# A two-layer encoder trunk: last query tile's 528 scores in one two-bank PSUM tile, 16-column meta scores, and a rearranged end of layer A

## The chip, the cores and the metric

One core of one Trainium2 chip runs the whole kernel in one launch. The metric is device time in microseconds; lower is better. The profile is one execution taken by the hardware profiler.

## The reference, cut to what matters

The input is 512 frames of 1024 features; 16 meta tokens are put in front, so L = 528. Layer A is differential attention (8 heads, two score maps a head, d = 64) and a conv-gated FFN; layer B is latent attention (16 heads, 64 plain and 32 rotary dimensions) and a second FFN. A frame sees its own chunk of 64 frames, the earlier chunks and the meta tokens; a meta token sees the 16 meta tokens alone.

```python
# layer A, per head                       # layer B, per head
a = softmax(q1 k1.T / 8)                  p = softmax((qn kn.T + qr kr.T) * 96**-0.5)
a = a - lam * softmax(q2 k2.T / 8)        o = p @ v
o = rms_norm(a @ v, g_sub) * (1 - lam_init)
h = h + concat(o) @ w_o;  h = h + conv_ffn(h)      # in both layers
```

## The kernel before, in words

Everything is float32. Each dense product is done in three TensorE passes of reduced-precision operands: every weight and activation is split into a high part (ScalarE, `act.copy`) and a low part (VectorE or GpSimd, a subtraction), and `mm3` (L162) issues high*high, high*low, low*high, each as a weight load and a matmul over 264 columns (half of L). Apart from stretches under `tc.manual_schedule`, the order of the instructions on each engine is not the program's: a planner goes through the program with its own estimate of durations and gives each engine, at each moment, the ready instruction of the highest priority, which is the earliest in the program (`soon(n)` moves a block n instructions forward). The order is fixed at build; on the chip each engine works through its queue in that order, and tiles that share a buffer wait for each other.

**Scores.** `scores` (L381) makes three steps for one head (layer B) or one map of a head (layer A). There are four query tiles of 128 rows, with 144, 272, 400 and 528 visible keys. The negated row maximum is a VectorE `tensor_reduce` (`negmax`, L391), the exponential a ScalarE `activation` that also returns the row sum (`ex`, L396). A PSUM bank holds 512 floats a partition, so the 528 keys of the last tile are cut in 256 and 272: `s0` puts tile 0 and the 256 in bank `b0`, the 272 in bank `b1`, joins the two maxima with a `min` (L410), and takes three exponentials; `s2` adds the two row sums (L428). `s1` puts the 400 keys of tile 2 in `b2` and, in its columns 400 to 415, the 16 meta scores: q of tokens 0 to 127 against the 16 meta keys, of which rows 0 to 15 are used. `s2` is tile 1 in `b3`. The four banks come from a pool of three (`psS`, tag "s"). One `qk` is two matmuls in layer A and three in layer B, each with its own weight load.

**Layer A's loop (L709).** For head h: `attend_a(h)` (scores of both maps, value projection `vproj(h)`, subtraction of the maps with L600, ten transposes L609 and four L623, values L630 and L631, squares and sums), then `qkproj(h + 1)`. `finish_a(h0, h1)` (L648) scales the outputs of heads h0 to h1-1 by their root mean square, transposes them and splits them into `oh` and `ol`. The root is on GpSimd (13 small instructions, `rsqrt`) where `soft` is true, else on ScalarE with Sqrt. `meta_soft_a` and `meta_a` do the meta tokens' rows. With KA = 5, `finish_a(4, 5)` stands after head 5 and `finish_a(5, 7)` after head 6; the meta rows go in groups of heads 0 to 3, 4, and 5 to 7. In the last head an activation with Sqrt on one column of the row sums (L588) stands ahead of `meta_soft_a(5, 3)`, which uses Exp, and `meta_a(5, 3)` stands at the end of `attend_a` (L639). ScalarE loads another table when the function changes between Exp and Sqrt.

**Output projection (L730).** Part 1 is the sum over heads 0 to KA-1 for the eight output tiles, in two halves each, 15 matmuls a PSUM bank; part 2 is heads KA to 7 and prepares the FFN's input tile by tile (L263). Both take banks from `psD`, which has two. Part 1 has the lowest priority of what surrounds it, so it fills TensorE where the attention leaves it free. `wload2` loads and splits weights for two output tiles at a time, in pieces of up to 512 columns.

Layer B (L1239) goes head by head: `s0`, values of head h-2, `s1`, transposes of head h-1, `s2`, with projections as fill.

Of the kernel before, what the change touches and what calls it, by code (L numbers as in the profile page):

```python
# [10 lines left out]
F32 = mybir.dt.float32  # L11
# [3 lines left out]
ALU = mybir.AluOpType  # L15
# [20 lines left out]
KA = KB = 5  # L36
# [21 lines left out]
def tile_trunk(ctx, tc, out, h0, gan0, small, w_qkv, a_w_o, kv_w_dkv, kv_w_ukv, b_w_dq, b_w_uq,  # L58
# [286 lines left out]
    first_ps = [[takeD() for _ in range(2)], [psS.tile([P, 512], F32, tag="s", name="psk") for _ in range(2)]]  # L345
# [35 lines left out]
    def scores(psS, ap_, parts, row, smeta, ebufs=2):  # L381
# [5 lines left out]
        def qk(ps, q0, k0, n):  # L387
            for i, (q, k) in enumerate(parts):
                pe.matmul(ps, q[:, q0:q0 + P], k[:, k0:k0 + n], start=i == 0, stop=i == len(parts) - 1)  # L389
# [9 lines left out]
        bank = lambda n: psS.tile([P, 512], F32, tag="s", name=n)  # L399

        def s0():
            b0 = bank("b0")
            qk(b0[:, 0:256], 16, 0, 256)
            qk(b0[:, 256:512], 400, 0, 256)
            negmax(b0[:, 0:144], 0, 80)
            negmax(b0[:, 256:512], 3)
            b1 = bank("b1")
            qk(b1[:, 0:272], 400, 256, 272)
            negmax(b1[:, 0:272], 4, 208)
            dve.tensor_tensor(nm[:, 3:4], nm[:, 3:4], nm[:, 4:5], ALU.min)  # L410
            ex(b0[:, 0:144], J0[0], 0, 0)
            ex(b0[:, 256:512], J0[3], 3, 3)
            ex(b1[:, 0:272], J0[3] + 256, 3, 4)

        def s1():
            b2 = bank("b2")
            qk(b2[:, 0:400], 272, 0, 400)
            qk(b2[:, 400:416], 0, 0, NM)
            negmax(b2[:, 0:400], 2, 336)
            dve.tensor_copy(smeta[:, row, :], b2[:NM, 400:416])  # L420
            ex(b2[:, 0:400], J0[2], 2, 2)

        def s2():
# [4 lines left out]
            dve.tensor_tensor(su[:, 3:4], su[:, 3:4], su[:, 4:5], ALU.add)  # L428
# [55 lines left out]
    some = iter([psT.tile([P, 512], F32, tag="t", name="psr"), psS.tile([P, 512], F32, tag="s", name="psr")])  # L484
# [92 lines left out]
    def attend_a(h, qs, ks, kl, vs0=None):  # L577
# [8 lines left out]
        if h == HA - 1:  # L586

            act.activation(s1a[:, 0, 0:1], es[1][1][:, 3:4], AF.Sqrt)  # L588
            ms = meta_soft_a(KA, 8 - KA)
# [8 lines left out]
        for j in (0, 3, 2, 1):  # L598
            sl = slice(J0[j], J0[j] + JN[j])
            dve.scalar_tensor_tensor(e1[:, sl], e2[:, sl], cc[:, j:j + 1], e1[:, sl], ALU.mult, ALU.add)  # L600

# [36 lines left out]
        if h == HA - 1:  # L638
            meta_a(KA, 8 - KA, *ms, soft=False)  # L639

# [68 lines left out]
    for h in range(HA):  # L709
# [8 lines left out]
        if h == 5:  # L718
            finish_a(4, KA)
            meta_a(4, KA - 4, *meta_soft_a(4, KA - 4))  # L720
        if h == 6:
            finish_a(KA, 7)
# [732 lines left out]
```

## Time and profile before

| | |
|---|---|
| median of 3 runs | 1312.9 us (1310.15 to 1313.72) |
| the profiled execution: time, span | 1312.65 us, 1310.8 us |
| TensorE matmul busy | 1279.3 us |
| VectorE, ScalarE, GpSimd busy | 814.4, 619.9, 206.1 us |
| layer A's attention, about | 36 to 297 us of the span |
| first FFN; latent products | 297 to 690; 690 to 737 us |
| layer B's attention and output | 737 to 938 us |
| second FFN and end | 938 to 1311 us |

Times are counted from the start of the span. PE is TensorE, PEld its weight loads (which overlap the matmuls), DVE VectorE, ACT ScalarE, POOL GpSimd. A matmul's record is longer than its pace: the distance from one start to the next says what it takes. The granted clock is 1.00 at 2.4 GHz and 0.50 at 1.2 GHz.

### The profile page before, as it was taken

The page shows a single profiled execution, that of the slowest core. Times are in us where ns is not written, and L with a number is a line of the kernel's source. Part 1 is how long each engine was busy: PE and PEld are TensorE (multiplying, and loading weights), DVE is VectorE, ACT ScalarE, POOL GpSimd, SP SyncE. Part 2 cuts the span into 40 slices and gives each one's busy share as a digit, 9 for nine tenths or more (in the row PEclk, how much of TensorE's full clock was granted, in tenths as well). Part 3 has the DMA queues.
Part 4 walks back from the last instruction along what each step waited for, and adds up shares of the span by engine and source line. Part 5 has one row for each costly group of instructions (what it writes and reads, how often), then busy time and mean ns, then how long its engine had stood idle before and what let it go on. Part 6 is the DMA issues. An engine that isn't in the chain of part 4 may idle for free.

```text
span 1310.8 us, 23833 instructions
## 1 busy us (share of the span) xinstructions
PE 1279.3 (98%) x9412; PEld 1212.6 (93%) x9412; DVE 814.4 (62%) x1702; ACT 619.9 (47%) x1319; POOL 206.1 (16%) x249
## 2 busy tenths in 40 slices
PE   9999999989999999999999899999999999999997
PEld 9899989989999999999999889999899999998886
DVE  6768887667666666533345778885866666662224
ACT  6666566555333433322234677874543333342223
POOL 5333541120000000000021644432200000000000
PEclk9999999989999999999999999999999999999999
DMA  6211211123233332333333545412332333332222
GB/s 211 82 54 56 71 53 49 57 73 100 82 97 90 88 97 82 92 89 90 89 109 62 120 101 122 116 43 81 98 96 87 92 97 97 96 100 92 87 93 81
DMA packets 166000, 117.13 MB, mean 89 GB/s; under 512 B 21248, under 2 KB 154688, under 8 KB 165888
## 3 DMA queue, kind: packets, MB, share of 16 engines
q1 hardware_dynamic: 165888, 115.61, 30.9%
q8 instruction: 74, 1.21, 0.4%
q14 instruction: 38, 0.31, 0.1%
HBM read 102.21 MB, written 2.10 MB: 80 GB/s over the span
## 4 chain that ended last, share of the span: by engine, by line
PE 76%; DVE 3%; ACT 2%; DMA 2%; POOL 1%; issue 1%; SPq 0%; ACTq 0%; POOLq 0%; DVEq 0%
PE psd L166 58%; PE psd L1357 9%; PE b L389 2%; PE ovb L1124 1%; PE tp L1091 1%; PE psd L1061 1%; DVE wlo L110 1%; DMA kt<-st 1%; PE ov L630 1%; DMA q<-st 0%; DVE nm L394 0%; PE tpm L1113 0%; ACT e L397 0%; ACT whi L109 0%; DVE xl L277 0%
## 5 line engine op out<-in xcount | busy, mean ns | idle before, releaser
L166 PE MATMUL psd<-xh,whi 128*128 128x264 f32 (+3 forms) x1664 | 494.2, 297 | 3.1 <-DVE qk L524 2.1
L166 PE MATMUL psd<-xh,wlo 128*128 128x264 f32 (+3 forms) x1664 | 493.1, 296 | 0.0
L166 PE MATMUL psd<-xl,whi 128*128 128x264 f32 (+3 forms) x1664 | 492.2, 296 | 0.7 <-DVE xl L349 0.5
L109 ACT CAST whi<-raw 128x512 fp32r<-128x512 f32 (+2 forms) x346 | 199.7, 589 | 378.7 <-PE psd L166 341.4
L166 PEld LDWEIGHTS psd<-xh,whi 128*128 128x128 f32 x1664 | 313.5, 189 | 12.3 <-DVE qk L524 2.8
L166 PEld LDWEIGHTS psd<-xl,whi 128*128 128x128 f32 x1664 | 313.5, 188 | 9.7 <-DVE xl L349 0.9
L166 PEld LDWEIGHTS psd<-xh,wlo 128*128 128x128 f32 x1664 | 313.4, 188 | 8.2 <-issue 0.4
L110 DVE TENSOR_TENSOR wlo<-raw,whi 128x512 fp32r<-128x512 f32 (+1 forms) x265 | 180.4, 686 | 129.2 <-ACT whi L109 128.0
L110 POOL TENSOR_TENSOR wlo<-raw,whi 128x512 fp32r<-128x512 f32 (+2 forms) x81 | 101.2, 1262 | 135.1 <-ACT whi L109 127.6
L166 PE MATMUL psd<-gh,whi 128*128 128x264 f32 x352 | 100.1, 285 | 0.0
L166 PE MATMUL psd<-gl,whi 128*128 128x264 f32 x352 | 99.9, 284 | 0.0
L166 PE MATMUL psd<-gh,wlo 128*128 128x264 f32 x352 | 99.8, 283 | 0.0
L397 ACT ACTIVATE e<-b,nm 128x272 f32<-128x272 f32 (+3 forms) x160 | 76.5, 481 | 33.5 <-DVE nm L394 19.2
L103 DVE TENSOR_TENSOR wlo<-raw,whi 128x512 fp32r<-128x512 f32 x44 | 28.7, 689 | 86.2 <-ACT whi L102 86.2
L131 POOL TENSOR_TENSOR raw<-raw,smalls 128x1024 f32<-128x1024 f32 x5 | 10.1, 2012 | 384.3 <-DVE acc L251 369.2
L260 DVE TENSOR_TENSOR hT<-psd,hT 128x264 f32<-128x264 f32 (+1 forms) x80 | 33.6, 424 | 57.7 <-PE psd L166 57.6
L102 ACT CAST whi<-raw 128x512 fp32r<-128x512 f32 x44 | 25.4, 619 | 92.7 <-PE psd L1357 75.9
L166 PEld LDWEIGHTS psd<-gl,whi 128*128 128x128 f32 x352 | 66.3, 188 | 0.0
L166 PEld LDWEIGHTS psd<-gh,wlo 128*128 128x128 f32 x352 | 66.3, 188 | 0.0
L166 PEld LDWEIGHTS psd<-gh,whi 128*128 128x128 f32 x352 | 66.2, 188 | 0.0
L394 DVE TENSOR_REDUCE nm<-b 128x1 f32<-128x272 f32 (+3 forms) x160 | 63.7, 423 | 1.2
L761 DVE TENSOR_TENSOR apad<-psd,rt 128x264 f32<-128x264 f32 (+1 forms) x88 | 37.5, 429 | 41.6 <-PE psd L166 41.6
(340 smaller groups left out, 2385.5 us busy)
## 6 DMA issues: line engine op xcount, KB each, us to landing
raw<-in_ffn_w_in SPq DMA_DIRECT2D x88, 512.0 KB
raw<-in_ffn_w_out SPq DMA_DIRECT2D x38, 512.0 KB
raw<-in_w_qkv SPq DMA_DIRECT2D x21, 512.0 KB
q<-st SPq DMA_DIRECT2D x28, 132.0 KB
kt<-st SPq DMA_DIRECT2D x28, 132.0 KB
raw<-in_ffn_w_out SPq DMA_DIRECT2D x8, 384.0 KB
hT<-in_h SPq DMA_DIRECT2D x8, 264.0 KB
q<-y SPq DMA_DIRECT2D x32, 66.0 KB
```

What stands on the lines that cost most here:

```text
L102: act.copy(hi, src)
L103: dve.tensor_tensor(lo, src, hi, ALU.subtract)
L109: act.copy(hi, src)
L110: wlo_engine[0].tensor_tensor(lo, src, hi, ALU.subtract)
L166: pe.matmul(ps[:rows, :n], a, xx[:, t0:t0 + n], start=first and ci == 0, stop=last and ci == 2)
L260: dve.tensor_tensor(hT[:, m, a:a + w], ps[:, :w], hT[:, m, a:a + w], ALU.add)
L389: pe.matmul(ps, q[:, q0:q0 + P], k[:, k0:k0 + n], start=i == 0, stop=i == len(parts) - 1)
L394: dve.tensor_reduce(nm[:, c:c + 1], ps, AX.X, ALU.max, negate=True)
L397: act.activation(e[:, o:o + ps.shape[1]], ps, AF.Exp, bias=nm[:, j:j + 1], accum_out=su[:, c:c + 1])
L630: pe.matmul(ov[:, j, :], ts[j][:, b * P:(b + 1) * P], vs[:, b, :], start=b == 0, stop=False)
L761: dve.tensor_tensor(a[:, off:off + n], ps[:, :n], rt[:, t0:t0 + n], ALU.mult)
L1357: pe.matmul(pso[t][n], a, ws[n][b], start=k == 0 and ci == 0, stop=k == NF - 1 and ci == 2)
```

## The change

The 528 scores get one PSUM tile of 1024 floats (two neighbouring banks, tag "s2", one buffer): 256 of its columns for tile 0 (144 used), then 528 columns, whose matmuls are still cut at the bank's border, one maximum over 528 columns and one exponential of 528. `b2` and `b3` share the one bank that is left. The meta scores are a product of 16 query rows (16 weight columns in place of 128). KA becomes 6 in layer A (KB stays 5; `finish_a` keeps its groups 4, and 5 to 6), so part 1 of the output projection sums six heads and part 2 two, and the meta groups are heads 0 to 3, 4 to 5, and 6 to 7. In the last head `meta_soft_a` goes ahead of the activation with Sqrt, which now reads all four row sums, and `meta_a` goes from the end of `attend_a` to behind L600.

```diff
-KA = KB = 5
+KA, KB = 6, 5
...
-    first_ps = [..., [psS.tile([P, 512], F32, tag="s", name="psk") for _ in range(2)]]
+    psk = psS.tile([P, 1024], F32, tag="s2", name="psk", bufs=1)
+    first_ps = [..., [psk[:, i * 512:(i + 1) * 512] for i in range(2)]]
...
-        def qk(ps, q0, k0, n):
+        def qk(ps, q0, k0, n, nq=P):
             for i, (q, k) in enumerate(parts):
-                pe.matmul(ps, q[:, q0:q0 + P], k[:, k0:k0 + n], ...)
+                pe.matmul(ps, q[:, q0:q0 + nq], k[:, k0:k0 + n], ...)
...
-        bank = lambda n: psS.tile([P, 512], F32, tag="s", name=n)
+        bank = lambda n: psS.tile([P, 512], F32, tag="s", name=n, bufs=NS - 2)
         def s0():
-            b0 = bank("b0")
+            b0 = psS.tile([P, 1024], F32, tag="s2", name="b0", bufs=1)
             qk(b0[:, 0:256], 16, 0, 256)
             qk(b0[:, 256:512], 400, 0, 256)
+            qk(b0[:, 512:784], 400, 256, 272)
             negmax(b0[:, 0:144], 0, 80)
-            negmax(b0[:, 256:512], 3)
-            b1 = bank("b1")
-            qk(b1[:, 0:272], 400, 256, 272)
-            negmax(b1[:, 0:272], 4, 208)
-            dve.tensor_tensor(nm[:, 3:4], nm[:, 3:4], nm[:, 4:5], ALU.min)
+            negmax(b0[:, 256:784], 3, 464)
             ex(b0[:, 0:144], J0[0], 0, 0)
-            ex(b0[:, 256:512], J0[3], 3, 3)
-            ex(b1[:, 0:272], J0[3] + 256, 3, 4)
+            ex(b0[:, 256:784], J0[3], 3, 3)
         def s1():
-            qk(b2[:, 400:416], 0, 0, NM)
+            qk(b2[:NM, 400:416], 0, 0, NM, NM)
         def s2():
-            dve.tensor_tensor(su[:, 3:4], su[:, 3:4], su[:, 4:5], ALU.add)
...
         if h == HA - 1:
-            act.activation(s1a[:, 0, 0:1], es[1][1][:, 3:4], AF.Sqrt)
             ms = meta_soft_a(KA, 8 - KA)
+            act.activation(s1a[:, 0, :], es[1][1][:, 0:4], AF.Sqrt)
...
             dve.scalar_tensor_tensor(e1[:, sl], e2[:, sl], cc[:, j:j + 1], e1[:, sl], ...)
+        if h == HA - 1:
+            meta_a(KA, 8 - KA, *ms, soft=False)
...
         osb_s[h] = osb
-        if h == HA - 1:
-            meta_a(KA, 8 - KA, *ms, soft=False)
...
         if h == 5:
-            finish_a(4, KA)
+            finish_a(4, 5)
             meta_a(4, KA - 4, *meta_soft_a(4, KA - 4))
         if h == 6:
-            finish_a(KA, 7)
+            finish_a(5, 7)
```

## Rows read from the trace of the kernel before

**Rows 1.** The page's first part: busy time, share, instructions of each engine.

```profile
PE 1279.3 (98%) x9412; PEld 1212.6 (93%) x9412; DVE 814.4 (62%) x1702; ACT 619.9 (47%) x1319; POOL 206.1 (16%) x249
```

**Rows 2.** Waits of the matmuls: us in total, times, longest.

```profile
PE psv L465 <- DVE om L703: 3.7, 1, 3.7
PE p L609 <- DVE e L600: 3.3, 4, 0.9
PE psd L166 <- DVE hT L260: 2.6, 3, 2.1
```

**Rows 3.** Stretches: length, then PE, PEld, DVE, ACT, POOL busy; clock, DMA.

```profile
61.00:64.00 3.00, 3.00 (x17) 3.00 (x17) 1.62 (x8) 1.97 (x8) 0.00 (x0) 0.54 0.46 168
...
221.70:240.40 18.70, 18.70 (x159) 18.62 (x157) 13.14 (x37) 10.07 (x25) 3.81 (x13) 1.00 0.22 72
...
248.25:250.40 2.15, 0.02 (x2) 0.02 (x1) 2.15 (x9) 1.16 (x5) 0.00 (x0) 1.00 0.00 0
...
267.50:271.30 3.80, 0.05 (x2) 0.02 (x1) 3.06 (x9) 2.17 (x5) 0.00 (x0) 0.76 0.38 110
271.30:276.30 5.00, 5.00 (x24) 4.96 (x25) 1.02 (x2) 0.99 (x2) 0.00 (x0) 0.50 0.34 100
...
800.00:850.00 50.00, 49.17 (x394) 46.27 (x393) 43.63 (x141) 41.22 (x125) 19.59 (x20) 1.00 0.50 113
```

**Rows 4.** ScalarE in order of time, layer A's end: start, length.

```profile
243.34 1.28 ACT L588 ACT_TABLE_LOAD   x1
...
267.71 1.28 ACT L645 ACT_TABLE_LOAD   x1
```

**Rows 5.** The same stretches, matmuls that read tile oh only: PE busy (count), clock.

```profile
221.70:240.40 18.70, 13.71 (x69) 1.00 0.22 72
```

**Rows 6.** GpSimd in order of time: first and last of 13, `finish_a(5, 7)`'s root.

```profile
233.22 0.20 POOL L204 TENSOR_SCALAR fr<-fv 128x8 int32<-128x8 int32 x1 [18.87 <-DVE fv L658]
...
237.82 0.20 POOL L209 TENSOR_TENSOR fr<-fr,rst 128x8 f32<-128x8 f32 x1
```

**Rows 7.** Weight loads in order of time, behind a meta product of layer A.

```profile
231.90 0.19 PEld L389 LDWEIGHTS b<-kl,qs 128*128 128x128 f32 x1
232.01 0.19 PEld L166 LDWEIGHTS psd<-oh,whi 128*128 128x128 f32 x1
```

**Rows 8.** Weight loads by shape: count, busy us, mean ns.

```profile
L389 PEld LDWEIGHTS b<-kt,q 96*128 96x128 f32 x288 | 41.0, 190 | 5.2 <-DMA kt<-st 2.1 <-ACT e L397 1.6 <-ACT st L102 1.2
...
L1113 PEld LDWEIGHTS tpm<-ident,e 128*16 128x16 f32 x64 | 5.2, 89 | 2.2 <-DVE of L1130 0.8 <-DVE ptl L103 0.3 <-issue 0.2
```

**Rows 9.** Matmuls in order of time, layer B.

```profile
829.43 0.94 PE L389 MATMUL b<-kt,q 96*128 96x400 f32 x6
...
830.77 0.35 PE L446 MATMUL psd<-ident,smetab 16*16 16x16 f32 x8
831.05 0.50 PE L1124 MATMUL ovb<-pth,vw 128*128 128x512 f32 x1
```

**Rows 10.** VectorE by shape: count, busy us, mean ns, idle before.

```profile
L394 DVE TENSOR_REDUCE nm<-b 128x1 f32<-128x272 f32 x64 | 27.5, 430 | 0.6
L394 DVE TENSOR_REDUCE nm<-b 128x1 f32<-128x400 f32 x32 | 18.1, 566 | 0.4
...
L410 DVE TENSOR_TENSOR nm<-nm 128x1 f32<-128x1 f32 x32 | 10.9, 342 | 0.3
L428 DVE TENSOR_TENSOR su<-su 128x1 f32<-128x1 f32 x32 | 6.4, 202 | 15.5 <-ACT e L397 15.3
```

**Rows 11.** Layer B, tile 2's exponential and tile 1's matmuls, in order of time.

```profile
816.59 0.62 PE L389 MATMUL b<-kt,q 96*128 96x272 f32 x3
...
817.12 0.58 ACT L397 ACTIVATE e<-b,nm 128x400 f32<-128x400 f32 x1
...
832.90 0.58 ACT L397 ACTIVATE e<-b,nm 128x400 f32<-128x400 f32 x1
...
834.91 1.72 PE L389 MATMUL b<-kt,q 96*128 96x272 f32 x12
```

More of the change, by code (lines that the diff above doesn't have):

```diff
@@ L344, in tile_trunk @@
     xh, xl = xtiles(xpool)
-    first_ps = [[takeD() for _ in range(2)], [psS.tile([P, 512], F32, tag="s", name="psk") for _ in range(2)]]
+    psk = psS.tile([P, 1024], F32, tag="s2", name="psk", bufs=1)
+    first_ps = [[takeD() for _ in range(2)], [psk[:, i * 512:(i + 1) * 512] for i in range(2)]]
     for k in range(KT):
@@ L385, in scores @@
         e = ap_.tile([P, PW], F32, tag="e", name="e", bufs=ebufs)
-        def qk(ps, q0, k0, n):
+        def qk(ps, q0, k0, n, nq=P):
             for i, (q, k) in enumerate(parts):
-                pe.matmul(ps, q[:, q0:q0 + P], k[:, k0:k0 + n], start=i == 0, stop=i == len(parts) - 1)
+                pe.matmul(ps, q[:, q0:q0 + nq], k[:, k0:k0 + n], start=i == 0, stop=i == len(parts) - 1)
         def negmax(ps, c, masked=None):
@@ L482, in tile_trunk @@
     sp.dma_start(smalls, small[:, :NGAIN + 132])
-    some = iter([psT.tile([P, 512], F32, tag="t", name="psr"), psS.tile([P, 512], F32, tag="s", name="psr")])
+    some = iter([psT.tile([P, 512], F32, tag="t", name="psr"), psS.tile([P, 512], F32, tag="s", name="psr", bufs=NS - 2)])
     with tc.manual_schedule(engines={mybir.EngineType.PE}):
```

## The prediction

> **What bounds the kernel now.** I read the page's first part, then the waits of the matmuls, then stretches with their granted clock, then the order of single instructions at the places that this led to. The first part shows TensorE busy for 1279.3 of 1310.8 us [rows 1]: 31.5 us is all that a faster VectorE or ScalarE could give back, and most of it lies at the kernel's two ends and in the latent products, which the change doesn't touch. So two things count: TensorE work that goes away, and TensorE's waits in layers A and B. The waits' list says where the latter are: the longest single one is 3.7 us before the transposes of the meta rows, one of 2.1 us is for an evacuation of the output projection, four before the last transposes of a head make 3.3 us [rows 2]. The stretches show that the first two lie at layer A's end, 248.25 to 250.40 (VectorE is busy throughout) and 267.50 to 271.30, and that the second is paid twice: the granted clock falls to 0.50, and the next 5.0 us of matmuls run at 1.2 GHz [rows 3]. ScalarE's order shows why both are there: three table loads of 1.28 us stand in that stretch, to Sqrt, back to Exp at 245.34, and to Sqrt again on the path of the last head's root (the first and the last in [rows 4]). In layer B TensorE has hardly a wait, 49.17 of 50 us busy, with VectorE at 43.63 and ScalarE at 41.22 close behind [rows 3].
>
> **Meta scores of 16 columns.** 80 weight loads shrink from 128 columns to 16: two in each of 16 maps of layer A, three in each of 16 heads of layer B. The first of each set hides under the 400-column matmul ahead of it; 16 + 32 = 48 are exposed, because a matmul of 16 columns covers nothing. Before, such a product lasts as long as its load: one load follows the other after 0.11 us [rows 7]. A 16-column load with a 16-column matmul is in the trace elsewhere: eight transposes from 830.77, the next matmul at 831.05, 0.035 us each [rows 9]. That gives 48 x 0.075 = 3.6 us on the engine that is the bound. From below it is nothing, if those places wait for something else anyway; from above it is the difference of the loads' records, 190 and 89 ns [rows 8], 48 x 0.101 = 4.8 us. I take 3.6, since a pace is nearer to what the path pays than a record. The Trainium skill (TensorE: Matmul & The Clock Gate, section LDWEIGHTS) counts a load as its columns divided by 1.2, in ns: 93 ns less for each, estimated 4.5 us in all, and 0.9 us less in the total than by the paces.
>
> **Layer A's end.** With `meta_soft_a` ahead of the Sqrt, and the Sqrt dependent on the last exponential, one switch is left of the three, and it lies off the path, where VectorE still joins the maps: two loads, 2.57 us of ScalarE, go. The wait of 2.13 us was an evacuation behind weight splits, and these behind ScalarE's casts, which the first two loads pushed back; the wait of 3.75 us holds the third load and then the root, the scaling and the meta rows one after the other. Moreover KA = 6 puts 48 more matmuls in part 1 and takes 6 of the 12 that part 2 can do ahead of head 7's result: 42 more as fill at that place. A matmul of 264 columns costs between 0.11 (the distance of loads [rows 7]) and 0.136 us (1279.3 us over 9412 [rows 1]); I take 0.12, so 5.0 us of fill against 3.75. All three parts of the loss, 2.13 + 3.75 + 5.0 x 0.5 for the clock = 8.4 us, can go; what is late next is TensorE itself.
>
> The other side is the middle. Part 1 now needs head 5, whose outputs come out of `finish_a(5, 7)` after head 6; before, it needed heads 0 to 4, ready long ago. From 221.70 to 240.40 TensorE did 69 matmuls with tile oh [rows 5], two of three passes, so 104 of part 1. With two banks only 2 x 15 = 30 can be done before head 5 is there; 74 x 0.12 = 8.9 us of fill is gone. Head 5's outputs wait for head 6's last sum and then for 13 GpSimd instructions, 233.22 to 238.02, 4.8 us [rows 6], and scaling, transposes and two evacuations follow. Not all is lost: the scores of head 7 stood behind fill in the same queue, and come sooner without it, and so does the root. I take half, 4.5 us of idle time, and for the clock what a broken stretch cost elsewhere: 0.54 granted for 3 us from 61 us on, behind three of the waits for L600 [rows 2, 3], 3 x 0.46 = 1.4 us. So 5.9 us lost, between nothing and 8.9 + 2.5 = 11.4. The end of layer A gains 8.4 - 5.9 = 2.5 us, between a loss of 3.0 and a gain of 8.4.
>
> `meta_a` moves with everything that it issues: four transposes, two products, some ten small VectorE instructions, three of ScalarE, no DMA; SP's queue and GpSimd's see nothing of it. It now takes three banks of `psT` ahead of the last head's transposes, which reuse them in turn, so the third tile of transposes waits until the meta rows are evacuated, and the last head's values queue behind. That costs nothing while part 1 fills (288 - 30 matmuls, some 31 us of them), and without that cover about the 3.7 us of [rows 2]. Weight splits: three and one pieces for a pair of output tiles in place of three and two, so four casts and four subtractions fewer, beside TensorE's work; the DMAs move the same bytes.
>
> **The 528 scores.** VectorE loses for each map two reduces, the `min` and the sum of the row sums, and gets one reduce of 528: 0.43 x 2 + 0.34 + 0.20 off, and 0.566 + 0.136 = 0.70 on (an estimate: 400 columns take 566 ns, 128 fewer take 136 less [rows 10]). 0.70 us a map, 22 us in all, and one exponential fewer on ScalarE. TensorE's matmuls are the same. As TensorE is the bound this is hidden, except where it waits for VectorE at the end of a map: the waits for L600 [rows 2]. I take one map's worth, 0.7 us; the bounds are nothing and the whole 3.3.
>
> **The sum**, against the profiled execution's own 1312.65 us (0.25 below the median of the three runs, too little to matter): 3.6 + 2.5 + 0.7 = 6.8 us off, **1306 us**.
>
> **Rivals.**
> *The middle eats the end (22%).* The planner finds nothing to put in place of the 74 matmuls: 11.4 lost against 8.4, and 1312.65 - 3.6 - 0.7 + 3.0 = 1311.3 us. For it: two banks are a hard limit, and the root on GpSimd can't be shortened. Against it: TensorE is busy for all of the 18.70 us from 221.70 on [rows 3], so the chains there have never been pressed, and what they can do is not seen.
>
> *Nothing is lost in the middle (15%).* Head 7's scores and value projection fill it: 1312.65 - 3.6 - 8.4 - 0.7 = 1300 us. For it: the value projection is 48 matmuls that the planner may place there. Against it: it has priority over part 1 and was used up before.
>
> *The banks wait (12%), slower than before.* `b2` and `b3` share one bank, so tile 1's matmuls wait for tile 2's exponential in every head. In layer B that exponential comes late: in one head it ended at 817.70 when tile 1's matmuls had begun at 816.59, 1.11 us sooner than one bank would allow [rows 11]. If each of 16 heads paid that, 17.8 us: 1312.65 - 6.8 + 17.8 = 1323.6 us. For it: ScalarE and VectorE are over 80% busy there, and their queues run in order. Against it: another head has the exponential done at 833.48 and the matmuls at 834.91 [rows 11], so this order fits already, and the planner knows of the shared bank. It decides from (6.8 + 3.9) / 16 = 0.67 us a head.
> The Trainium skill (PSUM — Partial Sum Buffer, section PSUM bank collisions raise a hardware error) adds that two engines may not be in one bank at once, even at other columns. By that tile 0's exponential has to wait for the maximum over 528, 0.27 us more than for one of 272 by the durations above; 32 times that is 8.6 us, and if all of it fell on TensorE, 1314.5 us. No row above singles it out.
>
> *The short loads don't show (8%).* Those places wait for something else, or the load has a floor: 1306 + 3.6 = 1309.6 us.
>
> **How the numbers follow.** The forecast has 43%, with a range of its own of 1303 to 1309. Its neighbours reach down to 1300 and up to 1311; the range for eight in ten is 1299.5 to 1313, which leaves out the banks' case and some tails. A measurement of this kernel tells 0.3%, 3.9 us, from no change. Faster than 1309: nearly all of the forecast, the second rival, two fifths of the last and a little of the first, 61%. Within 0.3%: most of the first and the rest of the last, 27%. Slower: the banks, 12%.
>
> **What would show it.** Right: one table load in ScalarE's order at layer A's end; no wait over 1 us before the meta rows, and the clock at 1.00 there; the 16-column products at under 0.06 us each; part 1 with some 30 matmuls ahead of head 5's outputs and waits of TensorE between 222 and 240 us that make about 4.5 us. Wrong: a fall of the clock near 235 us for longer than 3 us; a wait of `b3` for `e` in every head of layer B; layer B's stretch longer than before.

## The result and the profile after

The changed kernel takes 1327.05 us (median of 4 runs, 1326.22 to 1330.62) against 1313.31 us (1310.15 to 1317.10, 4 runs). Ratio 1.0104, 95% interval [1.0079, 1.0128]: slower by 1%, where 1306 us and faster was forecast, and outside the range. The profiled spans are 1324.4 and 1310.8 us.

Two marks in the chain of waits split the span: the four matmuls that add up the squares after layer A's output projection (I call their start *layer A's end*), and the same four after layer B's.

| | before | after | difference |
|---|---|---|---|
| layer A's end | 302.71 | 320.24 | +17.5 |
| from there to layer B's end | 634.2 | 630.2 | -4.0 |
| rest | 373.9 | 373.9 | 0 |

The first part of the page of after [rows 1]: the same 9412 matmuls, and VectorE and ScalarE have less to do.

```profile
PE 1280.9 (97%) x9412; PEld 1209.1 (91%) x9412; DVE 811.7 (61%) x1602; ACT 609.5 (46%) x1249; POOL 205.9 (16%) x249
```

The waits of the matmuls from 34 to 300 us of after (us in total, times, longest) [rows 2]. Before's wait of 3.7 for om and that of 2.1 for hT are gone from layer A's end: the 1.2 for om here stands at 205.46, before the first meta group's transposes, and the 1.2 for hT at 258.12, in the middle. Three new ones stand at the top, and all end with a VectorE instruction.

```profile
PE b L390 <- DVE qs L539: 6.6, 1, 6.6
PE p L609 <- DVE e L597: 5.2, 2, 4.5
PE psd L166 <- DVE qk L521: 4.8, 3, 3.1
PE b L390 <- ACT e L398: 3.3, 2, 2.6
PE psd L166 <- DVE hT L260: 1.8, 2, 1.2
PE psv L462 <- DVE om L701: 1.2, 1, 1.2
```

Stretches of after, read as in [rows 3] (length; PE, PEld, DVE, ACT, POOL busy; clock; DMA). The first three are the new waits: TensorE does nothing and VectorE is busy throughout. The fourth shows the second price, 1.2 GHz. The next four are the middle, around the sixth head's outputs. Then comes the end of part 1, where before's two losses lay, and layer B's stretch.

```profile
110.08:114.58 4.50, 0.00 (x0) 0.03 (x1) 4.50 (x5) 0.00 (x0) 2.85 (x2) 1.00 0.12 21
170.10:173.16 3.06, 0.00 (x1) 0.01 (x1) 3.06 (x5) 0.86 (x2) 1.74 (x2) 0.91 0.50 169
195.18:201.78 6.60, 0.01 (x1) 0.04 (x1) 6.47 (x11) 4.17 (x7) 5.92 (x10) 0.86 0.12 40
201.78:206.78 5.00, 3.78 (x18) 3.29 (x19) 4.16 (x14) 0.55 (x2) 4.10 (x12) 0.50 0.01 3
...
244.00:249.00 5.00, 3.06 (x25) 2.66 (x24) 2.97 (x12) 3.16 (x12) 1.17 (x6) 1.00 0.01 2
249.00:254.00 5.00, 2.69 (x12) 2.48 (x13) 3.65 (x18) 2.50 (x9) 1.46 (x8) 0.71 0.00 0
254.00:259.00 5.00, 3.27 (x17) 2.77 (x16) 4.45 (x13) 2.67 (x6) 0.00 (x0) 0.50 0.00 0
259.00:264.00 5.00, 5.00 (x32) 4.61 (x32) 0.84 (x2) 0.60 (x2) 0.00 (x0) 0.76 0.00 0
...
295.00:300.00 5.00, 4.38 (x34) 4.02 (x34) 3.10 (x6) 2.22 (x4) 0.00 (x0) 1.00 0.46 133
800.00:850.00 50.00, 47.27 (x367) 42.35 (x366) 41.56 (x111) 37.90 (x106) 20.36 (x22) 1.00 0.54 125
```

Matmuls of after up to the wait of the middle that read tile oh [rows 5], and in the second row those that read tile ol: 20 and 10, which make the 30 of part 1 that were forecast as the most, since two of three passes read oh and the third reads ol.

```profile
200.00:250.40 50.40, 4.14 (x20) 3.25 (x20) 1.19 (x3) 1.29 (x3) 0.90 0.13 39
...
200.00:250.40 50.40, 2.85 (x10) 1.88 (x10) 1.19 (x3) 0.90 0.13 39
```

ScalarE of after at layer A's end has one table load [rows 4].

```profile
254.73 1.28 ACT L586 ACT_TABLE_LOAD   x1
```

Weight loads of the meta products of after by shape (count, busy us, mean ns) [rows 8]: 95 to 98 ns where 128 columns took 190.

```profile
L390 PEld LDWEIGHTS b<-kt,q 96*16 96x16 f32 x48 | 3.5, 95 | 1.3
L390 PEld LDWEIGHTS b<-ks,qs 128*16 128x16 f32 x16 | 1.6, 98 | 0.0
```

VectorE's maxima of after by shape [rows 10]: the maximum over 528 takes 695 ns, where 0.70 us was estimated.

```profile
L395 DVE TENSOR_REDUCE nm<-b 128x1 f32<-128x528 f32 x32 | 22.2, 695 | 0.5
L395 DVE TENSOR_REDUCE nm<-b 128x1 f32<-128x400 f32 x32 | 18.2, 568 | 0.5
```

Waits of the matmuls of after from 737 to 945 us, layer B. The row that the shared bank would show: twice, 0.7 us together, where the rival "the banks wait" asked for over 1 us in each of 16 heads [rows 11].

```profile
PE b L390 <- ACT e L398: 0.7, 2, 0.4
```

So the loss is in layer A, for the most part before the stretch that the prediction looked at, and it is no work. Adding 5-us windows from 34 to 304 us, TensorE is idle for 25.2 us (before 12.9), and its busy time at less than full clock (in each window the busy time times one minus the granted clock) is worth another 9.8 us (before 3.8): 18.3 us more in sum, for the 17.5 by which layer A's end is later.

### The profile page after: what moved, and what is told of

Same layout as the page of the kernel before. It is cut to its first block, busy times and chain, and to the rows that moved or that the text cites. A ratio compares the mean times of both kernels' runs of the same rounds, so it can differ in the third digit from the quotient of the medians.

```text
span 1324.4 us, 23667 instructions
## 1 busy us (share of the span) xinstructions
PE 1280.9 (97%) x9412; PEld 1209.1 (91%) x9412; DVE 811.7 (61%) x1602; ACT 609.5 (46%) x1249; POOL 205.9 (16%) x249
## 3 DMA queue, kind: packets, MB, share of 16 engines
q8 instruction: 74, 1.21, 0.4%
## 4 chain that ended last, share of the span: by engine, by line
PE 81%; DVE 8%; ACT 4%; DMA 2%; issue 2%; POOL 2%; SPq 1%; DVEq 0%; ACTq 0%; POOLq 0%
PE psd L166 62%; PE psd L1355 9%; PE b L390 2%; PE ov L630 1%; PE ovb L1122 1%; DMA sw<-qkraw 1%; DVE nm L395 1%; ACT whi L109 1%; PE tp L1089 1%; DVE ptl L103 1%; PE p L609 1%; PE ov L631 1%; ACT e L398 1%; DVE e L597 1%; DVE osb L663 0%
## 5 line engine op out<-in xcount | busy, mean ns | idle before, releaser
L166 PEld LDWEIGHTS psd<-xh,whi 128*128 128x128 f32 x1664 | 313.4, 189 | 14.6 <-DVE qk L521 5.5
L110 POOL TENSOR_TENSOR wlo<-raw,whi 128x512 fp32r<-128x512 f32 (+2 forms) x81 | 97.9, 1219 | 150.4 <-ACT whi L109 145.6
L398 ACT ACTIVATE e<-b,nm 128x144 f32<-128x144 f32 (+3 forms) x128 | 68.4, 537 | 37.9 <-DVE smeta L418 16.0
L260 DVE TENSOR_TENSOR hT<-psd,hT 128x264 f32<-128x264 f32 (+2 forms) x80 | 33.7, 424 | 61.1 <-PE psd L166 60.6
L395 DVE TENSOR_REDUCE nm<-b 128x1 f32<-128x144 f32 (+3 forms) x128 | 62.9, 497 | 2.0
```

Source lines behind the costliest of these rows:

```text
L110: wlo_engine[0].tensor_tensor(lo, src, hi, ALU.subtract)
L166: pe.matmul(ps[:rows, :n], a, xx[:, t0:t0 + n], start=first and ci == 0, stop=last and ci == 2)
L260: dve.tensor_tensor(hT[:, m, a:a + w], ps[:, :w], hT[:, m, a:a + w], ALU.add)
L395: dve.tensor_reduce(nm[:, c:c + 1], ps, AX.X, ALU.max, negate=True)
L398: act.activation(e[:, o:o + ps.shape[1]], ps, AF.Exp, bias=nm[:, j:j + 1], accum_out=su[:, c:c + 1])
```

## The experiments

Each table row: ratio to before with its 95% interval, layer A's end, and its idle time plus clock loss from 34 to 304 us, by the same windows. Layer A's end less that loss is 284 to 287 us in every run: layer A is a nearly fixed amount of TensorE work, and its end is later by what is lost. Layer A's end and the loss come from one profiled execution of each kernel. The diffs are cut to the lines that count, and partly written short.

| run | ratio | A's end | idle + clock |
|---|---|---|---|
| before | | 302.7 | 12.9 + 3.8 |
| after | 1.0104 [1.0079, 1.0128] | 320.2 | 25.2 + 9.8 |
| e1_narrowA | 0.9994 [0.9982, 1.0006] | 305.8 | 15.4 + 5.4 |
| e2_ka5 | 1.0068 [1.0045, 1.0092] | 315.7 | 21.3 + 9.9 |
| e3_meta16 | 0.9956 [0.9940, 0.9973] | 301.4 | 12.8 + 4.5 |
| e4_end | 1.0000 [0.9985, 1.0016] | 302.1 | 11.7 + 3.3 |
| e5_fixedA | 1.0016 [1.0002, 1.0029] | 301.9 | 14.0 + 2.7 |
| e6_wideA | 1.0115 [1.0099, 1.0131] | 314.2 | 20.2 + 7.7 |
| e7_pair | 0.9912 [0.9896, 0.9928] | 290.4 | 4.7 + 0 |
| e8_end5_16 | 0.9959 [0.9945, 0.9972] | 301.5 | 12.4 + 3.0 |
| e9_holdA | 1.0060 [1.0039, 1.0080] | 309.6 | 17.1 + 6.3 |
| e10_wide4 | 1.0105 [1.0084, 1.0125] | 315.4 | 21.2 + 7.7 |
| e11_pairA | 0.9879 [0.9865, 0.9894] | 291.2 | 5.0 + 0 |
| e12_pairA_end5 | 0.9936 [0.9919, 0.9952] | 298.5 | 9.4 + 3.2 |
| e13_wideA_late | 1.0042 [1.0019, 1.0065] | 306.9 | 15.5 + 5.3 |
| e14_before_late | 1.0024 [1.0011, 1.0036] | 304.6 | 14.4 + 4.0 |
| e15_after_dve | 1.0036 [1.0025, 1.0047] | 311.2 | 19.7 + 6.0 |
| e16_before_dve | 0.9979 [0.9967, 0.9991] | 298.3 | 8.4 + 3.6 |
| e17_after_dve_late | 1.0057 [1.0040, 1.0074] | 312.7 | 20.1 + 6.3 |
| e18_pairA_dve | 0.9848 [0.9833, 0.9862] | 285.4 | 1.2 + 0 |

### Which part of the change it is

**e1_narrowA**: the changed kernel with layer A's scores in three narrow banks, as before.

```diff
 def scores(...)                 # layer A: wide=False, layer B: as changed
+    b0, b1 = bank("b0"), bank("b1")     # 256 and 272 keys, two maxima, min
-    b0 = psS.tile([P, 1024], F32, tag="s2", name="b0", bufs=1)
```

> The changed kernel with layer A's scores back in three single banks (256 + 272 with min and sum); everything else of the change stays (528 in two banks in layer B, 16-column meta scores, KA = 6, layer A's end). Banks theory (the shared banks stretch the score phases of layer A's heads, so TensorE waits for VectorE in heads 2 to 5): the waits of 4.5 us near 110, 3.1 us near 170 and 6.6 us near 195 go, the wait near 250 stays; 1309 to 1314 us. KA theory (only KA = 6 costs): about the changed kernel's 1327 us. Order theory (any edit makes the planner lay out layer A anew, none of the parts is at fault): other waits of that size at other places, 1316 to 1327 us.

Measured 1313.27 us: the loss is gone, and with it the waits near 110, 170 and 195 us. Layer A's end moves by 14.4 us, so the 528 scores in layer A are what costs. The order theory has a part in it too: two other waits have come, 3.50 us at 223.74 and 6.88 us at 240.94. In layer B the wide scores stay, and nothing is lost there.

**e2_ka5**: the changed kernel with KA = 5.

```diff
-KA, KB = 6, 5
+KA, KB = 5, 5
```

> The changed kernel with KA = 5 (meta groups of heads 0 to 3, 4, and 5 to 7 as before the change); all else of the change stays. Banks theory: the waits in heads 2 to 5 (14 us with the clock's falls) stay, the one near 250 us goes: 1320 to 1324 us. KA theory: 1308 to 1311 us. Order theory: anything between 1308 and 1327 us with the waits at other places.

1322.55 us: KA = 6 is 4.6 us of the changed kernel's A's end, and the greater part of the loss stays without it.

**e3_meta16**: before, with the 16-column meta scores alone (the two `qk` lines of the change's diff).

```diff
-            qk(b2[:, 400:416], 0, 0, NM)
+            qk(b2[:NM, 400:416], 0, 0, NM, NM)
```

> The kernel before with nothing but the 16-column meta scores. By the paces of the weight loads 3.6 us less than before (about 1309.5 us), if layer A's order stays; the 16-column products at under 0.06 us each. If the short loads have a floor or those places wait for something else: no change. Order theory: layer A changes by several us either way although no work was added.

A gain of 0.44%, 5.8 us (0.27 to 0.60%, 3.5 to 7.9 us); 3.6 was forecast, at the lower edge of that.

**e4_end**: before, with KA = 6 and layer A's end rearranged.

```diff
-KA = KB = 5
+KA, KB = 6, 5
+ms = meta_soft_a(...); act.activation(s1a[:, 0, :], ..., AF.Sqrt)   # this order
+meta_a(...)                                  # behind L600
```

> The kernel before with KA = 6 and layer A's end rearranged (meta_soft_a ahead of the Sqrt, meta_a behind the joining of the maps), scores in three banks and meta scores of 128 columns. Forecast of the prediction's second term: 2.5 us less than before (bounds: 3.0 more, 8.4 less). Banks theory: between these bounds, no wait over 2 us in heads 2 to 5. KA theory: 10 us or more above before.

Ratio 1.0000 (0.9985 to 1.0016), layer A's end 0.6 us sooner: what the tail wins the middle loses for the most part, and 2.5 us of gain were too many.

**e6_wideA**: before, with the wide scores in layer A alone.

```diff
-            b0 = bank("b0"); ...; b1 = bank("b1")
+            b0 = psS.tile([P, 1024], F32, tag="s2", name="b0", bufs=1)
+            negmax(b0[:, 256:784], 3, 464); ex(b0[:, 256:784], J0[3], 3, 3)
-    bank: bufs=NS
+    bank: bufs=NS - 2          # b2 and b3 share one
```

> The kernel before with the 528 scores in two banks in layer A alone (one maximum, one exponential; b2 and b3 share a bank); meta scores of 128 columns, KA = 5, layer B and layer A's end as before. One-bank theory: 1322 to 1328 us, as with the fixed banks, less at most 2 us for the instructions saved. If it takes the whole change together: 1311 to 1316 us.

1.0115: this part alone makes the whole loss, 15 us of the time and 11.5 us of A's end. The rest of the 15 lies in the stretch from A's end to B's, where the edit changes nothing: 638.1 us here and 634.2 before, which is the least of the nine kernels with 128-column meta scores (the others take 636.5 to 639.1).

**e8_end5_16**: e3 with the end rearranged, KA = 5.

```diff
+ms = meta_soft_a(...); act.activation(s1a[:, 0, :], ..., AF.Sqrt); meta_a(...) behind L600
```

> The kernel before with 16-column meta scores and layer A's end rearranged (one table load), KA = 5: no fill is lost in the middle. If the prediction's account of the end is right, the waits of 2.1 and 3.7 us and the fall of the clock go and nothing takes their place: 1301 to 1305 us. If the end is bound by the last head's own chain, other waits come in their place: 1306 to 1310 us, as with the meta scores alone.

0.9959 beside e3's 0.9956: the rearrangement without KA = 6 is worth nothing either. As the expectation's second case had it, other waits come: 2.11 us for om at 259.01 and 2.99 us for osb at 269.32.

### What about the two-bank tile costs

**e5_fixedA**: before, layer A's `b0` and `b1` each with a bank of its own, `b2` and `b3` in the third, nothing wide.

```diff
-bank = lambda n: psS.tile([P, 512], F32, tag="s", name=n)
+psS.tile([P, 512], F32, tag={"b0": "s0", "b1": "s1"}.get(n, "s"), name=n, bufs=1)
```

> The kernel before, with one edit in layer A: its three banks no longer rotate; the bank of tile 0 and the 256 columns and the bank of the 272 belong to these alone, and tiles 2 and 1 (b2, b3) share the third. No instruction is wider or fewer. If the one bank that b2 and b3 share stretches the score phases (four turns a head through it, each some 5 us of matmul, maximum and exponential), this costs layer A nearly what the change did: 1322 to 1328 us, score phases of 17 to 25 us a head in place of 12 to 17. If the 528-wide maximum and exponential or the two-bank tile itself are at fault: 1311 to 1315 us.

A's end 301.9: one bank for `b2` and `b3` is not the cause. A head's scores take 15.8 to 28.1 us from first to last matmul here (before 12.6 to 17.6), so a long turn of the scores is not the cause either.

**e9_holdA**: e6, but the two-bank tile keeps the narrow instructions (two maxima, `min`, three exponentials): only its being taken and released as one is left.

```diff
             b0 = psS.tile([P, 1024], F32, tag="s2", name="b0", bufs=1)
-            negmax(b0[:, 256:784], 3, 464)
+            negmax(b0[:, 256:512], 3); negmax(b0[:, 512:784], 4, 208); min
```

> Layer A's scores as in the run with the wide scores in layer A alone (two-bank tile, b2 and b3 in one bank), but with the narrow instructions of before in it: two maxima, their min, exponentials of 256 and 272, the sum. It differs from the fixed banks (no loss) only in that the two banks are taken and given back together, and from the wide scores (15 us lost) only in the instructions. If giving back the two banks together is what costs: 1322 to 1330 us, idle time and clock loss of layer A near 28 us. If the wide maximum and exponential cost (a longer hold of VectorE and ScalarE, tile 0's exponential behind the 528): 1311 to 1317 us, near 17 us.

A's end is at 309.6 us, 6.9 of the 11.5, between the two cases of the expectation: being taken and released as one costs by itself, and the rest comes with the wide instructions.

**e10_wide4**: e6 with a bank each for `b2` and `b3` and one bank fewer for the transposes.

```diff
-    psT, psTst = open_pool("psT", NT, space=PSUM)
+    psT, psTst = open_pool("psT", 2, space=PSUM)
-bank: bufs=NS - 2
+bank: bufs=2
```

> The wide scores in layer A alone, with four banks for the scores: the two-bank tile, and one bank each in turn for b2 and b3; the transposes' pool gives up its third bank for it. If the loss needs both the two-bank tile and a shared bank for b2 and b3: 1309 to 1316 us, near 17 us of idle time and clock loss in layer A (or better, if fewer instructions help). If the two-bank hold alone costs, or the third transpose bank is needed: 1322 us or more.

A head's scores take 8.0 to 12.2 us now, less than before, and the loss is as large, 12.7 us. So a bank each for `b2` and `b3` does not cure it; what the bank taken from the transposes costs was not tried by itself. Its waits from 34 to 300 us say where it lies: in the transposes of the meta rows.

```profile
PE psv L477 <- DVE om L715: 12.6, 3, 5.2
```

**e7_pair**: a new packing in both layers, with e3's meta scores: tiles 1 and 0 in one bank, tiles 2 and 3 and the meta scores in one two-bank tile, with single maxima and exponentials.

```diff
+b0 = psS.tile([P, 512], ...);  qk(b0[:, 0:272], 144, 0, 272); qk(b0[:, 272:416], 16, 0, 144)
+b2 = psS.tile([P, 1024], ...); qk(b2[:, 0:400], 272, 0, 400)
+qk(b2[:, 400:512], 400, 0, 112); qk(b2[:, 512:928], 400, 112, 416)
+negmax(b2[:, 400:928], 3, 464); ex(b2[:, 400:928], J0[3], 3, 3)
```

> The kernel before with 16-column meta scores and another packing of the same three banks in both layers: the two-bank tile holds tile 2's 400 columns, tile 3's 528 (112 of them in the first bank, 416 in the second) and the meta scores, the single bank holds tiles 0 and 1 (144 + 272). Each map takes each buffer once, so a head of layer A needs two turns of each in place of four through one bank; one maximum and one exponential of 528 as in the change. One-bank theory: score phases back to 10 to 16 us a head, 1303 to 1309 us, no slower than the 16-column meta scores alone. If two-bank tiles are at fault: 1318 us or more.

A's end 290.4, 12.3 us sooner than before. So neither a two-bank tile nor instructions over 528 columns cost by themselves. From A's end to B's it takes 636.0 us, where the other ten runs with 16-column meta scores take 629.7 to 632.6, so in layer B the packing loses some 4 us.

**e11_pairA** has that packing in layer A alone, the old banks in layer B; **e12_pairA_end5** has layer A's end rearranged besides.

```diff
-scores(psS, ab, ..., h, smeta)                      # layer B: e7
+scores(psS, ab, ..., h, smeta, paired=False)        # layer B: e11, e12
```

> The new packing (tiles 2 and 3 and the meta scores in the two-bank tile, tiles 0 and 1 in the single bank) in layer A alone; layer B with its three single banks and 16-column meta scores. In the run with the packing in both layers, layer A gained 12.3 us and the stretch from the end of layer A's attention to the end of layer B's took 636 us against 632 with the meta scores alone. If the packing costs layer B these 4 us: 1297 to 1300 us; if the stretch varies by that anyway: 1300 to 1304 us.

> The same with layer A's end rearranged (meta_soft_a ahead of the Sqrt, meta_a behind the joining), KA = 5. With the packing the waits at layer A's end are gone already, so little is left for the end to give: within 2 us of the packing in layer A alone. If the table loads still cost something: 2 to 4 us less.

1298.64 and 1305.70 us: e11 as expected, e12 a miss. In e11 the waits of [rows 2] at layer A's end are gone with KA = 5 and the old order there; in e12 the rearranged end brings one back (3.0 us for osb, clock 0.50) and costs 7.3 us of A's end. The edit that won 0.6 us of it in e4 and changed it by 0.2 in e8 loses 7.3 here.

### Why TensorE waits

In the trace of e6, matmuls in order of time: a projection's last matmul at 192.96, then the four transposes of the first meta group, which wait 4.97 us for om, then four more transposes, then scores that wait too.

```profile
192.85 0.28 PE L166 MATMUL psd<-xl,whi 128*128 128x264 f32 x1
192.96 0.28 PE L166 MATMUL psd<-xh,wlo 128*128 128x264 f32 x1
198.22 0.60 PE L477 MATMUL psv<-ident,om 16*128 16x16 f32 x4 [4.97 <-DVE om L715]
198.75 1.11 PE L577 MATMUL pv<-ident,acc 128*128 128x128 f32 x4
...
200.96 0.89 PE L390 MATMUL b<-ks,qs 128*128 128x256 f32 x2 [0.88 <-DVE qs L554]
```

om is the end of a chain of small VectorE instructions and 13 of GpSimd that begins with eight TensorE products of the meta values. TensorE's order is fixed, so if the chain is late, all that stands behind the transposes waits too. Before, the same transposes come without a wait; the wait ahead of them is for qk, another tile.

```profile
188.51 0.39 PE L166 MATMUL psd<-xh,whi 128*128 128x264 f32 x1 [1.51 <-DVE qk L524]
...
191.76 0.42 PE L465 MATMUL psv<-ident,om 16*128 16x16 f32 x4
```

The stretch from the first of the eight products to the first transpose, before and in e6, read as [rows 3]:

```profile
177.85:191.76 13.91, 12.35 (x97) 11.61 (x97) 11.83 (x32) 6.11 (x20) 7.63 (x18) 1.00 0.19 49
...
183.64:198.22 14.58, 9.61 (x78) 9.09 (x77) 10.77 (x21) 6.17 (x16) 10.50 (x19) 0.94 0.21 54
```

The chain takes about as long in both, 13.9 and 14.6 us. Counted in TensorE's order (the windows above also count what reaches into them) the transposes have not moved: the first is the kernel's matmul 1468 in both. The eight products have: they begin at matmul 1372 before and at 1392 in e6, so the new order leaves 76 matmuls to cover the chain in place of 96. The count alone does not settle it: e9 has 91, and waits 4.21 us. In e6 single steps of the chain are also drawn out beside GpSimd's subtractions: the chain's own instruction at L711 takes 1.17 us (0.14 before), and one of the 13 on GpSimd 1.21 where most take 0.19.

```profile
187.97 1.17 DVE L711 SCALAR_TENSOR_TENSOR mv<-ms,mv 16x4 f32<-16x4 f32 x1
...
193.69 1.21 POOL L209 TENSOR_TENSOR mr<-mr,rst 16x4 f32<-16x4 f32 x1
```

Against before the whole chain is 0.7 us longer, so most of the 4.97 us comes from its later beginning. What the chain would take in e6 without GpSimd's subtractions was not tried; before, with them on VectorE (e16 below), it takes 11.2 us, from 176.61 to 187.84.

**e13_wideA_late**: e6, with these transposes and their two evacuations issued one head later; **e14_before_late** is the control, before with the same.

```diff
-        meta_out(takeT, om, oh, ol, h0, n, gsub)
+        f = lambda: meta_out(takeT, om, oh, ol, h0, n, gsub)
+        f() if h0 else later.append(f)
...
         if h == 5:
+            later.pop()()
             finish_a(4, KA)
```

> The kernel before with the two-bank 528 scores in layer A only (measured 1.0115 of before, layer A's end at 314.24 us), and of the first meta group (heads 0 to 3) the four transposes and their two evacuations issued one head later, behind head 5. In its trace TensorE waits 4.97 us at 198 us in these transposes for om, then 0.88 us for head 5's scores, then runs at half clock. Theory 'queue': the loss is work whose operands come late standing in TensorE's fixed order ahead of work that is ready; then about 5 us of waits and 2 to 3 us of clock go, layer A's end near 306 to 308 us, ratio 1.005 to 1.007. Rival 'no fill': the scores' longer turn eats the fill, and the idle time only moves to the next wait; then layer A's end stays at 312 to 316 us, ratio 1.010 to 1.013.

> Control: the kernel before with the same four transposes one head later. Before, that wait is 1.51 us at 188.5 us. Theory 'queue': at most 1.5 us less, ratio 0.998 to 1.001. Rival 'no fill': nothing changes, 1.000. If it gains more than 4 us, the place of these transposes costs the kernel before as well, and the first comparison says nothing about the 528 scores.

e13: A's end 306.9 (306 to 308 expected), ratio 1.0042 where 1.0115 stood, 0.73% or 9.6 us less. e14, the control: 1.0024, a loss of 3 us, where at most a small gain was expected. The 1.51 us that its expectation names are the wait for qk above; before, these transposes have no wait to lose, so the control shows that issuing them later is no gain by itself. With the transposes late, the wide scores cost 1.0042 / 1.0024 = 0.18%, 2.4 us, and the two intervals overlap; with the transposes early they cost 1.15%, 15 us. The same place in the trace of e13: TensorE goes on with products, and the meta transposes come at 201.97 without a wait.

```profile
192.90 0.28 PE L166 MATMUL psd<-xh,whi 128*128 128x264 f32 x1
193.02 0.28 PE L166 MATMUL psd<-xl,whi 128*128 128x264 f32 x1
193.14 0.28 PE L166 MATMUL psd<-xh,wlo 128*128 128x264 f32 x1
...
196.54 1.25 PE L621 MATMUL p<-ident,e 128*128 128x128 f32 x10
198.68 0.39 PE L166 MATMUL psd<-xh,whi 128*128 128x264 f32 x1 [0.89 <-DVE mv L709]
...
201.97 0.42 PE L477 MATMUL psv<-ident,om 16*128 16x16 f32 x4
```

The changed kernel's longest wait, 195.18 to 201.78, is for head 5's rotated q (qs, L539). VectorE of after in order of time shows what is ahead of it in its queue.

```profile
192.98 1.26 DVE L532 TENSOR_TENSOR sw<-sw,sr 80x1056 f32<-80x1056 f32 x1
194.16 0.17 DVE L681 TENSOR_TENSOR mt<-smeta,mc 16x32 f32<-16x32 f32 x1
194.26 0.67 DVE L694 TENSOR_REDUCE ms<-omq 16x4 f32<-16x512 f32 x1
194.86 0.15 DVE L591 RECIPROCAL cc<-su 128x4 f32<-128x4 f32 x1
194.94 1.22 DVE L533 TENSOR_TENSOR qk<-qk,sw 80x1056 f32<-80x1056 f32 x1
196.09 1.24 DVE L682 TENSOR_TENSOR mt<-mt,smeta 16x32 f32<-16x32 f32 x1
197.26 1.26 DVE L697 SCALAR_TENSOR_TENSOR mv<-ms,mv 16x4 f32<-16x4 f32 x1
...
198.89 2.01 DVE L597 SCALAR_TENSOR_TENSOR e<-e,cc 128x144 f32<-128x144 f32 x4
200.93 0.70 DVE L539 SCALAR_TENSOR_TENSOR qs<-qk,qs 64x528 fp32r<-64x528 f32 x1
```

Two instructions on 16 rows take 1.24 and 1.26 us, and GpSimd of after computes low weight parts at that time:

```profile
194.40 4.11 POOL L110 TENSOR_TENSOR wlo<-raw,whi 128x512 fp32r<-128x512 f32 x2 [4.74 <-ACT whi L109]
198.61 0.19 POOL L204 TENSOR_SCALAR mr<-mv 16x4 int32<-16x4 int32 x1
```

The same two lines of after in another shape, by shape, take 211 and 138 ns:

```profile
L682 DVE TENSOR_TENSOR mt<-mt,smeta 16x64 f32<-16x64 f32 x1 | 0.2, 211 | 0.0
L697 DVE SCALAR_TENSOR_TENSOR mv<-ms,mv 16x2 f32<-16x2 f32 x2 | 0.3, 138 | 0.0
```

**e15_after_dve**: the changed kernel with layer A's subtractions of weights on VectorE; **e16_before_dve**, the control, before with the same; **e18_pairA_dve**, e11 with it.

```diff
-    wlo_engine[0] = pool
     nxt = qkproj(0)
```

> The changed kernel with layer A's low weight parts computed on VectorE instead of GpSimd. In the changed kernel's trace the three long waits of the middle (4.51 us at 114.6, 3.06 at 173.2, 6.59 at 201.8) each stand behind small VectorE operations that take 1.2 us and more while GpSimd runs a 128x512 subtraction, about 9 us more than the same operations take elsewhere. Theory 'shared slowdown': these waits shrink by about that and some clock comes back, layer A's end near 308 to 311 us, ratio 1.000 to 1.004. Rival 'no fill': VectorE gets some 31 subtractions of about 0.7 us more, the chains get no shorter, and layer A's end is 318 to 325 us, ratio 1.009 to 1.014.

> Control: the kernel before with layer A's low weight parts on VectorE. Its trace shows as much VectorE time lost beside GpSimd (16 us against 12 in the changed kernel) and only 12.9 us of idle TensorE. Theory 'shared slowdown': little to win, since fill covers it, ratio 0.996 to 1.001. Rival 'no fill': VectorE's added 20 us press on the chains, ratio 1.001 to 1.006.

e15: A's end 311.2, 9.0 us sooner, as expected, though VectorE now has GpSimd's subtractions to do. But the control's A's end is 4.4 us sooner too (0.9979, in its range), so of A's end half of the 9 is the kernel's own; of the time it is 2.8 us of 8.9. 1.0036 / 0.9979 leaves 0.57% to the change, where 1.04% stood.

**e17_after_dve_late**: the changed kernel with both edits.

```diff
-    wlo_engine[0] = pool
+    later = []                     # and the edit of e13
```

> The changed kernel with both edits: layer A's low weight parts on VectorE, and the first meta group's four transposes one head later. With the first edit alone layer A's end is at 311.22 us (ratio 1.0036), and TensorE still waits 3.38 us at 197.3 in these transposes, behind 1.40 and 2.33 us of waits of head 5's scores for an exponential. Theory 'queue and slowdown': what is left of the loss in the middle goes, some 3.4 us and 1 to 2 us of clock; layer A's end 306 to 308 us, ratio 0.999 to 1.001, near the 305.82 us that the changed kernel has with layer A's old scores. Rival 'no fill': the wait moves to the next operation with a late operand and layer A's end stays at 310 to 313 us, ratio 1.003 to 1.006.

A miss: 312.7 us, as the rival had it. TensorE no longer waits at 197, but 3.21 us for om at 227.98, and its longest wait from 34 to 300 us is now in the middle, before `finish_a(5, 7)`'s transposes:

```profile
PE po L666 <- DVE osb L663: 7.0, 1, 7.0
```

e1 has the same wait at the same place, 6.88 us at 240.94. It is the middle that KA = 6 makes late; the changed kernel has five smaller waits there. What one edit gives back, the next late operand can take again.

> The fastest version so far (two-bank tiles packed in pairs in layer A, 16-column meta scores; ratio 0.9879, layer A's end 291.17 us, 5.0 us of TensorE idle in layer A and no clock lost) with layer A's low weight parts on VectorE. Theory 'queue and slowdown': nothing waits there, so taking the slowdown away wins at most the 5.0 us of idle time; ratio 0.985 to 0.989, layer A's end 288 to 292 us. Rival 'no fill': VectorE's added work makes it late somewhere, layer A's end 294 us or more, ratio 0.990 or more.

e18: 1293.08 us (1291.38 to 1294.19), the fastest version, 1.52%, about 20 us, under before. A's end is 5.8 us sooner than e11's; at most 5.0 was expected, and idle time gave 3.8 of it. Its first part of the page, and its only wait of over 0.25 us from 34 to 300:

```profile
PE 1271.2 (98%) x9412; PEld 1203.2 (93%) x9412; DVE 819.5 (63%) x1696; ACT 611.0 (47%) x1285; POOL 137.4 (11%) x207
```

```profile
PE psd L166 <- DVE qk L549: 0.9, 1, 0.9
```

GpSimd has 59 us less to do than in e11 (196.6), VectorE only 5.1 more (814.4).

## Why the prediction was wrong

**What failed** is the step "The 528 scores", with its sentence "As TensorE is the bound this is hidden, except where it waits for VectorE at the end of a map". It was put at 0.7 us of gain; it measured 11.5 us of loss in layer A by itself (e6) and 14.4 in the changed kernel (after against e1). The reduces cost what was estimated, and TensorE's work is the same. By the sum of their records the forecast's 22 us of VectorE are saved, but its busy time falls by 2.7 us only (814.4 to 811.7), since the records that went overlapped others and the other instructions took longer. Above all, the step priced the instructions and took the order for given. The order of layer A is planned anew when a buffer changes. What the new order lost, the runs show for e6: transposes whose operand comes late stand ahead of ready work, because the chain to that operand begins later in TensorE's order (moving the transposes takes out 9.6 of 15 us, while the same move costs before 3 us).

The sum of the profiled spans by terms, forecast against measured:

| | forecast | measured |
|---|---|---|
| 528 scores in layer A | -0.7 | +14.4 (A's end, after less e1) |
| layer A's end, and meta scores in layer A | -2.5 - 1.2 | +3.1 (A's end, e1 less before) |
| layer B: 32 meta loads | -2.4 | -4.0 |
| sum | -6.8 | +13.5 (spans: +13.6) |

The second row missed as well, by 6.8 us; the two paragraphs on layer A's end below say where.

**Meta scores**: right in sign and mechanism. Forecast were 3.6 us, measured 5.8 (3.5 to 7.9), so the forecast lies at the lower edge of what was measured. From A's end to B's the ten runs with the short loads, e7 aside, take 629.7 to 632.6 us and the nine with the long ones 634.2 to 639.1; the means, 631.4 and 637.1, are 5.7 us apart where 2.4 was forecast for layer B. Taking idle time and clock loss out of this stretch as above leaves 3.3 us, near the records' difference for the 32 loads there (94 ns each, 3.0 us); the other 2.4 us are less idle time and clock loss, and why they come was not tried. The wide scores in layer B add nothing: the five runs that have them (after, e1, e2, e15, e17) take 629.7 to 632.3.

**Layer A's end, the tail**: right in its mechanism together with KA = 6. One table load is left; from 295 to 300 us the clock is at 1.00 and 0.62 us of one wait remain. In e4 the 8.4 us that before loses from 244 to 279 us (6.1 idle, 2.3 of clock) are down to 0.3. Without KA = 6 the same rearrangement brings other waits (e8, e12), so the saved table loads alone did not free the end. The meta rows, though, now stand in the middle, beside a clock of 0.50.

**Layer A's end, the middle**: the mechanism was right, and the count too: part 1 did the 30 matmuls that two banks allow. The size does not hold from one order to the next. In e4, from 229 to 244 us, 3.0 us of idle time and 3.3 of clock are lost, 6.2 in sum where 5.9 were taken. In after, from 244 to 264 us, the waits are 0.69, 2.65, 0.91, 0.57 and 1.16, 6.0 us, and the clock adds 2.69 x 0.29 + 3.27 x 0.5 + 5.00 x 0.24 = 3.6: 9.6 us, inside the bound of 11.4, and more than the tail's 8.4, as the first rival had it for this part. In e1, from 219 to 249 us, 11.0 us of idle time and 5.4 of clock are lost, 16.4 in sum and outside the bound. This is where the table's second row misses.

**The rival on the slower side** had the shared bank in layer B. Its place was wrong: layer B got shorter, so neither the shared bank nor a longer wait of tile 0's exponential shows there. e5 shows that in layer A such a sharing costs 0.3% at most, and A's end is no later with it.

**What stays open.** Why a tile taken and released as one (e9: 6.9 us of 11.5) leads to an order with late operands in front, and the same two banks packed otherwise (e7, e11) to one with next to none, is not shown. Nor is how much of e6's loss GpSimd's subtractions make. In the changed kernel itself the two cures don't add up (e17), so no list of causes for its 14.4 us is complete: what is shown is that it is idle time and clock, in which waits it lies, and that e15's edit takes 9.0 us off it, 4.4 of which before gains as well.

## What to carry to other kernels

Where the order of each engine is fixed at build, an edit of a buffer's size is an edit of the order: price it with bounds as wide as the fill it can use up (here the same three banks in other layouts gave 10 us less, e11 against e3, and 11.5 more, e6 against before), and not by its instructions. When a stage is bound by one engine, write its end as work plus idle plus clock loss; the first is constant here to 1.6 us either way over 20 kernels, so each run shows at once what there is to win. Issue work whose operand is the end of a long chain of small instructions a step later than the code suggests, with a control: the same edit cost before 3 us.

## What the runs showed of the hardware

VectorE and GpSimd hold each other up. Beside GpSimd's 128x512 subtractions a VectorE instruction with two tensor operands on 16x4 elements took 1.26 us (L697 in after), the same one before 0.14, while a sum (L694, 0.67) and a reciprocal (L591, 0.15), with one operand each, took no longer there than elsewhere. Two scalings of 128x512 took 3.40 us at 110.08 in after, beside two subtractions on GpSimd from 110.00 to 112.93; in e6 one takes 0.69 at 204.67. GpSimd's own two took 4.11 us from 194.40 in after, and a single one 1.28 at 185.79 in e6. The Trainium skill (SBUF — State Buffer, section SBUF: two separate sides) states this as a lock: a VectorE instruction with two SBUF inputs and a GpSimd instruction that reads SBUF take a shared pair of ports in turn, each for its whole length. These rows agree with it, the ones with one operand too. The prediction gave it no price.

The clock fell behind some waits of TensorE and not behind others. In after the 5 us behind the waits of 4.50, 3.06 and 6.60 us ran at a granted clock of 0.66, 0.71 and 0.50; before, the 5 us behind the wait of 2.15 us that ends at 250.40 ran at 1.00, and those behind the wait of 3.80 us that ends at 271.30 at 0.50 [rows 3]. In e11 and e18, where the longest waits are 1.34 and 0.94 us, every 5-us window from 34 to 304 us shows 1.00.
